# Splitting 16 rows off the second load of a single-core transpose, into two transfers of 8 rows

## The chip, the cores and the metric

The kernel runs on one core of a Trainium2 chip. The metric is the device time of one execution in microseconds (us). The kernel before was run twice: 1261.91 and 1262.47 us, median 1262.19 us. A profiled execution of the same kernel is read below; its span, from the first to the last instruction of the program, is 1260.4 us.

## The reference

```python
def setup_inputs():
    return {"x": np.random.randn(8192, 8192).astype(np.float32)}

def reference(x):
    return np.transpose(x)
```

The input has 8192 x 8192 float32 values, 268.4 MB. All of it is read once from HBM and all of it written once, transposed.

## The kernel before

**Tiling.** The input is cut into 128 chunks. Chunk t is a pair (s, c): s is one of two halves of 4096 columns, c one of 64 blocks of 128 rows. A chunk is a tile of 128 partitions with 4096 float32 each; one row of it in one partition has 16 KB, the whole tile 2 MB. `load(t)` (L101) brings it into one of three input buffers, `ins[t % 3]`. The first three loads are issued on SyncE's queue, all later ones on ScalarE's queue (L103).

**Transposing.** For each chunk TensorE does 32 transposes of 128 x 128 (`transposes`, L112), in eight groups q of four. The first four groups land in the first half of PSUM, the last four in the second half. A group takes every fourth column, so partition p of the result holds four neighbouring rows of the output. TensorE runs this as a loop in hardware registers (L130 to L140).

**Copying and storing.** ScalarE copies the first half of PSUM and VectorE the second half into one of nine regions of `regs` in SBUF (L241). A region is a window of up to eight chunks for one q: 128 partitions, four output rows each, up to 1024 columns, so 2 MB when full. Windows are staggered (L198), so that from the start one window closes with each chunk; the first ones and the last ones are shorter. A closed window is stored by `store` (L154), always from ScalarE's queue; every store but the first goes through the helper `wide_dma` (L25), which builds the transfer by hand.

**What orders the work.** Each engine has its own stream, and semaphores tie them. `s_ld[k]` (one for each input buffer) gets 16 from a landed load, one increment for each transfer engine, and one each from ScalarE's and VectorE's last copy of the chunk before. TensorE takes a chunk when it reads 18 and subtracts 18 (L113). For chunk 0 the two copies are replaced by plain increments (L96, L97). `s_pe` counts TensorE's progress for the copies and for ScalarE, which issues the store of a closed window and then `load(t + 3)` into the buffer that TensorE has finished. `s_st[r]` counts the landed stores of region r; a copy that opens a new window waits for it. At the end SyncE waits for the stores of all nine regions (L266).

Of the kernel before, what the change touches and what calls it, by code (L numbers as in the profile page):

```python
# [8 lines left out]
def physical(ap):  # L9


    t = ap.tensor
    dims = [list(d) for d in ap.ap]
    if len(dims) == 2:
        dims.insert(1, [dims[1][1], 1])
    return mybir.PhysicalAccessPattern(
        ap=dims,
        offset=ap.offset,
        dtype=ap.dtype,
        memref=t.name,  # L20
        memsetref=t.name + "_set",
    )


def wide_dma(nc, eng, queue, out, in_):  # L25


    return eng.add_instruction(
        mybir.InstDMACopy(
            mode="Copy",  # L30
            name=nc.get_next_instruction_name(),
            engine=eng.engine,
            ins=[physical(in_)],
            outs=[physical(out)],
            queue=queue,
        )
    )
# [3 lines left out]
def kernel(  # L41
# [13 lines left out]
    nc = tc.nc  # L55
    P = 128
# [8 lines left out]
    NIN = 3  # L65
    NREG = 9
    CH = N // P
    J = S * P

    with tc.tile_critical():  # L70
        nc.alloc_sbuf_tensor("pad", [P, 32], dt)
        ident = nc.alloc_sbuf_tensor("ident", [P, P], dt).ap()
        ins = [nc.alloc_sbuf_tensor(f"in{k}", [P, J], dt).ap() for k in range(NIN)]
        SIZE = B * W * P
# [4 lines left out]
        s_id = nc.alloc_semaphore("s_id")  # L79
        s_ld = [nc.alloc_semaphore(f"s_ld{k}") for k in range(NIN)]  # L80
        s_st = [nc.alloc_semaphore(f"s_st{k}") for k in range(NREG)]
        s_pe = nc.alloc_semaphore("s_pe")
        s_cp = [nc.alloc_semaphore("s_cpa"), nc.alloc_semaphore("s_cpv")]

# [3 lines left out]
            out=ident,  # L88
            in_=ident,
# [8 lines left out]

        chunks = [(s, c) for s in range(M // J) for c in range(CH)]

        def load(t):  # L101
            s, c = chunks[t]
            (nc.sync if t < NIN else nc.scalar).dma_start(  # L103
                out=ins[t % NIN], in_=x[c * P:(c + 1) * P, s * J:(s + 1) * J]
            ).then_inc(s_ld[t % NIN], 16)

# [34 lines left out]
        for t in range(NIN):  # L143
            load(t)

        copied = [0, 0]
        free = list(range(NREG))
        stored = [0] * NREG
        window = {}

        def later(t):
            return W <= t < T - NIN

        def store(q, e, t):  # L154
            t0, r, parts = window.pop(q)
            if later(t):
                nc.scalar.wait_ge(s_pe, (t + 1) * NH + 1)
            else:
                nc.scalar.wait_ge(s_cp[e], copied[e])
            base = 0  # L160
            pieces = []
            for s, a, z in parts:
                rows = (z - a) * P
                j0 = s * J + q * B * P
                dst = out[j0:j0 + B * P, a * P:a * P + rows]
                dst = dst.rearrange("(q b) i -> q b i", q=P)
                src = regs[:, r * SIZE + base:r * SIZE + base + B * rows]
                base += B * rows
                pieces.append((rows, dst, src))
            for rows, dst, src in sorted(pieces, key=lambda v: -v[0]):  # L170
                if any(stored):
                    st = wide_dma(nc, nc.scalar, "qActDynamicHW", dst, src)
                else:
                    st = nc.scalar.dma_start(
                        out=dst, in_=src.rearrange("q (b i) -> q b i", b=B)
                    )
                st.then_inc(s_st[r], 16)
                stored[r] += 1
            free.append(r)

        def closes(w, t):
            t0, r, parts = w
            return t + 1 == t0 + sum(z - a for _, a, z in parts)

        for t, (s, c) in enumerate(chunks):
            closed = []
            for e in range(2):
                eng = (nc.scalar, nc.vector)[e]
                go = s_ld[(t + 1) % NIN]

                place = []
                fresh = {}
                for q in range(e * NH, (e + 1) * NH):
                    if q not in window:

                        span = (q - c) % W + 1  # L198
                        r = free.pop(0)
                        parts = [(s, c, min(c + span, CH))]  # L200
                        if c + span > CH and t + span < T:
                            parts.append((s + 1, 0, c + span - CH))
                        window[q] = (t, r, parts)
                        if stored[r]:
                            fresh[q - e * NH] = (s_st[r], 16 * stored[r])
                    t0, r, parts = window[q]
                    k = [p[0] for p in parts].index(s)
                    base = r * SIZE + B * P * sum(z - a for _, a, z in parts[:k])
                    _, a, z = parts[k]
                    place.append((base + (c - a) * P, (z - a) * P))  # L210

                runs = []
                for g in range(NH):
                    if runs:
                        u = runs[-1]
                        gap = place[g][0] - place[g - 1][0]
                        if place[g][1] == place[u[0]][1] and abs(gap) < 2 ** 15 and (
                            len(u) == 1 or gap == place[u[1]][0] - place[u[0]][0]
                        ):
                            u.append(g)  # L220
                            continue
                    runs.append([g])
                if later(t):
                    runs = sorted(runs, key=lambda u: any(g in fresh for g in u))
                seen = t * NH + e * NH // 2
                for u in runs:
                    off, dist = place[u[0]]
                    gap = place[u[-1]][0] - place[u[-2]][0] if len(u) > 1 else 0
                    dims = [list(regs.ap[0]), [gap, len(u)], [dist, B], [1, P]]
                    o = bass.AP(regs.tensor, regs.offset + off, dims)  # L230
                    i = pss[e][:, u[0] * B * P:(u[-1] + 1) * B * P]
                    i = i.rearrange("p (l b i) -> p l b i", b=B, i=P)
                    need = t * NH + (e * NH + u[-1]) // 2 + 1
                    if later(t) and u is runs[0] and len(runs) > 1 and any(g in fresh for g in runs[-1]):
                        need = t * NH + (e * NH + max(v[-1] for v in runs)) // 2 + 1
                    if need > seen:
                        eng.wait_ge(s_pe, need)
                        seen = need
                    for sem, value in [fresh[g] for g in u if g in fresh]:
                        eng.wait_ge(sem, value)  # L240
                    cp = nc.scalar.copy(out=o, in_=i) if e == 0 else nc.vector.tensor_copy(out=o, in_=i)  # L241
                    ends = [e * NH + g for g in u if closes(window[e * NH + g], t)]
                    if later(t):
                        if u is runs[-1]:
                            cp.then_inc(go, 1)
                        closed += [(q, e) for q in ends]
                        continue
                    if ends:
                        cp.then_inc(s_cp[e], 1)
                        copied[e] += 1  # L250
                    if u is runs[-1]:
                        if ends:
                            eng.wait_ge(s_cp[e], copied[e])
                            eng.sem_inc(go, 1)
                        else:
                            cp.then_inc(go, 1)
                    for q in ends:
                        store(q, e, t)
            for q, e in closed:
                store(q, e, t)  # L260
            if t + NIN < T:
                if not closed:
                    nc.scalar.wait_ge(s_pe, (t + 1) * NH)
                load(t + NIN)
        for r in range(NREG):
            nc.sync.wait_ge(s_st[r], 16 * stored[r])  # L266


# [28 lines left out]
```

## Time and profile before

| what | value |
|---|---|
| median of two runs | 1262.19 us (1261.91 to 1262.47) |
| span of the profiled execution | 1260.4 us |
| TensorE matmul busy | 739.0 us, 59% |
| VectorE busy | 302.0 us, 24% |
| ScalarE busy | 253.5 us, 20% |
| bytes moved by transfers | 536.95 MB, 426 GB/s over the span |
| ScalarE's transfer queue (q10) | 530.60 MB, 99.0% of 16 engines' span |
| SyncE's transfer queue (q1) | 6.29 MB, 1.2% |

The profiled execution has no time of its own beside its span; the span stands 1.8 us under the median of the runs, which time the whole execution from outside.

A profile row for a group of instructions reads: line, engine, operation, out<-in, count, then busy time and mean. A row of a table of stretches gives the stretch, its length, the busy time of each engine with its count of instructions, the granted TensorE clock, the mean busy share of the 16 transfer engines, and the GB/s moved. In that table a transfer packet is counted, whole, where it starts. A row of the timeline gives start, length, engine, line, operation and count, and in brackets how long the engine had been idle and what ended that. "ACTq" and "SPq" are the instruction queues of ScalarE and SyncE.

### The profile page before, as it was taken

How to read it: one execution, taken by the hardware profiler on the slowest of the kernel's cores; microseconds unless marked ns; L12 is line 12 of the kernel's file. 1: busy time of each engine (PE TensorE's matmuls, PEld its weight loads, DVE VectorE, ACT ScalarE, POOL GpSimd, SP SyncE). 2: the span in 40 equal slices, each digit the busy share in tenths (PEclk: the TensorE clock that was granted, in tenths of full speed). 3: DMA queues.
4: the chain of work that ended last, by engine and by line, in shares of the span. 5: the costliest groups of instructions: out<-in, count | busy, mean ns of one | idle time of the engine just before them, and what ended most of it. 6: DMA issues, size and time to landing. Idle time of an engine off the chain costs nothing. (4 is left out here: it accounts for less than half of the span.)

```text
span 1260.4 us, 9367 instructions
## 1 busy us (share of the span) xinstructions
PE 739.0 (59%) x4096; PEld 718.4 (57%) x4096; DVE 302.0 (24%) x250; ACT 253.5 (20%) x257; POOL 0.7 (0%) x6
## 2 busy tenths in 40 slices
PE   5656556565566655565556656566565655665561
PEld 5556556565556655565555656565565655665561
DVE  2322222222222222222222222222222222222220
ACT  3212211122111211122111211121111211121110
POOL 0000000000000000000000000000000000000000
PEclk9886876868777777778687786867777687777776
DMA  9999999999999999999999999999999999999998
GB/s 383 429 422 426 425 430 431 426 431 431 427 430 431 428 428 431 428 429 432 427 422 426 429 429 425 431 429 428 430 428 428 431 428 429 429 429 429 429 431 376
DMA packets 39271, 536.95 MB, mean 426 GB/s; under 512 B 4320, under 2 KB 4832, under 8 KB 6240
## 3 DMA queue, kind: packets, MB, share of 16 engines
q10 hardware_dynamic: 38832, 530.60, 99.0%
q1 hardware_dynamic: 432, 6.29, 1.2%
q14 instruction: 6, 0.05, 0.0%
q8 instruction: 1, 0.02, 0.0%
HBM read 268.44 MB, written 268.44 MB: 426 GB/s over the span
## 5 line engine op out<-in xcount | busy, mean ns | idle before, releaser
L117 PE MATMUL ps<-ident,in 128*128 128x128 f32 x4096 | 739.0, 362 | 493.5 <-PEq L113 493.5
L117 PEld LDWEIGHTS ps<-ident,in 128*128 128x128 f32 x4096 | 718.4, 220 | 513.9 <-issue 513.9
L241 DVE COPY regs<-ps 128x512 f32<-128x512 f32 (+3 forms) x250 | 302.0, 1246 | 932.1 <-PE ps L117 932.1
L241 ACT COPY regs<-ps 128x512 f32<-128x512 f32 (+3 forms) x256 | 252.2, 1016 | 978.8 <-PE ps L117 760.8
L241 ACT ACT_TABLE_LOAD x1 | 1.3, 1283 | 1.0 <-SPq L70 1.0
L87 POOL TENSOR_SCALAR_AFFINE_SELECT ident<-ident 128x128 f32<-128x128 f32 x1 | 0.3, 293 | 0.2 <-POOL ident L85 0.2
L85 POOL MEMSET ident<- 128x128 f32 x1 | 0.2, 204 | 0.5 <-SPq L70 0.5
L281 POOL MEMSET const-bfloat16-1.0<- 128x1 bf16 x1 | 0.1, 102 | 0.0
L281 POOL MEMSET const-uint8-127<- 128x1 uint8 x1 | 0.1, 102 | 0.0
L281 POOL MEMSET const-float32-0.0<- 128x1 f32 x1 | 0.1, 99 | 0.2 <-issue 0.2
L281 POOL MEMSET const-float32-1.0<- 128x1 f32 x1 | 0.1, 99 | 0.0
## 6 DMA issues: line engine op xcount, KB each, us to landing
in<-in_x_dram ACTq DMA_DIRECT2D x125, 2048.0 KB, 16.8
out_dram<-regs ACTq DMA_DIRECT2D x114, 2048.0 KB, 12.6
out_dram<-regs ACTq DMA_DIRECT2D x4, 1792.0 KB, 11.1
in<-in_x_dram SPq DMA_DIRECT2D x3, 2048.0 KB, 11.7
out_dram<-regs ACTq DMA_DIRECT2D x4, 1536.0 KB, 12.5
out_dram<-regs ACTq DMA_DIRECT2D x4, 1280.0 KB, 11.5
out_dram<-regs ACTq DMA_DIRECT2D x4, 1024.0 KB, 11.1
out_dram<-regs ACTq DMA_DIRECT2D x4, 768.0 KB, 12.3
```

The costliest lines, as they stand in the source:

```text
L85: nc.gpsimd.memset(ident, 0.0).then_inc(s_id, 1)
L87: nc.gpsimd.affine_select(out=ident, in_=ident, compare_op=mybir.AluOpType.not_equal, fill=1.0, base=0, pattern=[[-1, P]], channel_multipl ...
L117: tr = nc.tensor.transpose(pss[e][:, (g * B + b) * P:(g * B + b + 1) * P], ins[k][:, q * B * P + b:(q + 1) * B * P - B + b + 1:B], ident,)
L241: cp = nc.scalar.copy(out=o, in_=i) if e == 0 else nc.vector.tensor_copy(out=o, in_=i)
L281: nc = _bacc.Bacc("TRN2", target_bir_lowering=False, num_devices=1)
```

## The change

Only the load of chunk 1, one of the three that SyncE issues at the start, is cut. Its first 112 rows stay one transfer on SyncE's queue. Rows 112 to 119 go in a transfer on SyncE's queue, rows 120 to 127 in one on ScalarE's queue. Both are built by `wide_dma` with the source seen as 4 x 2 rows. They count on a semaphore of their own, `s_ex`. VectorE waits for 32 on it ahead of its last copy of chunk 0; the increment of that copy is one of those that TensorE needs before it takes chunk 1. Besides, the wait for the region stored last moves at the very end of the program from SyncE to VectorE.

```diff
+    EXTRA = [(4, 2), (4, 2)]
...
+        s_ex = nc.alloc_semaphore("s_ex")
...
         def load(t):
             s, c = chunks[t]
+            src = x[c * P:(c + 1) * P, s * J:(s + 1) * J]
+            a = P - sum(e * n for e, n in EXTRA) if t == 1 else P
             (nc.sync if t < NIN else nc.scalar).dma_start(
-                out=ins[t % NIN], in_=x[c * P:(c + 1) * P, s * J:(s + 1) * J]
+                out=ins[t % NIN][:a], in_=src[:a]
             ).then_inc(s_ld[t % NIN], 16)
+            if t == 1:
+                for (e, n), (eng, queue) in zip(EXTRA, ((nc.sync, "qSPDynamicHW"), (nc.scalar, "qActDynamicHW"))):
+                    part = src[a:a + e * n].rearrange("(e n) j -> e n j", e=e)
+                    wide_dma(nc, eng, queue, ins[t][a:a + e * n], part).then_inc(s_ex, 16)
+                    a += e * n
...
+                    if t == 0 and e == 1 and u is runs[-1]:
+                        eng.wait_ge(s_ex, 16 * len(EXTRA))
                     cp = nc.scalar.copy(out=o, in_=i) if e == 0 else nc.vector.tensor_copy(out=o, in_=i)
...
         for r in range(NREG):
-            nc.sync.wait_ge(s_st[r], 16 * stored[r])
+            (nc.vector if r == free[-1] else nc.sync).wait_ge(s_st[r], 16 * stored[r])
```

In the order of the built program, SyncE issues the load of chunk 0, the 112 rows, the first 8 rows, then the load of chunk 2. ScalarE issues the second 8 rows as its very first transfer, ahead of its function table load and its first copy. Nothing else moves on any engine.

## The prediction

> **What bounds the kernel now.** I read the page first: the span, the line of slices for the transfers, the queues and the transfer issues.
>
> ```profile
> span 1260.4 us, 9367 instructions
> ...
> DMA  9999999999999999999999999999999999999998
> ...
> q10 hardware_dynamic: 38832, 530.60, 99.0%
> q1 hardware_dynamic: 432, 6.29, 1.2%
> ...
> in<-in_x_dram ACTq DMA_DIRECT2D x125, 2048.0 KB, 16.8
> out_dram<-regs ACTq DMA_DIRECT2D x114, 2048.0 KB, 12.6
> ...
> in<-in_x_dram SPq DMA_DIRECT2D x3, 2048.0 KB, 11.7
> ```
>
> All 40 slices are full: the 16 transfer engines are busy from one end to the other, and 99.0% + 1.2% of their time is packets. A load lands 16.8 us after its issue, though 2 MB cost far less (next view): it stands behind other transfers. So the kernel is bound by its transfers, and the change neither adds nor removes a byte. What can move is which of the 16 engines carries which row. The next view is the table of stretches, for the middle and the last microseconds.
>
> ```profile
> 200.00:500.00 300.00, 182.52 (x992) 177.53 (x992) 72.60 (x54) 59.64 (x48) 0.00 (x0) 0.74 1.01 429
> ...
> 1255.12:1255.72 0.60, 0.00 (x0) 0.00 (x0) 0.00 (x0) 0.00 (x0) 0.00 (x0) 0.50 1.03 437
> 1255.72:1256.33 0.61, 0.00 (x0) 0.00 (x0) 0.00 (x0) 0.00 (x0) 0.00 (x0) 0.50 0.89 376
> 1256.33:1256.94 0.61, 0.00 (x0) 0.00 (x0) 0.00 (x0) 0.00 (x0) 0.00 (x0) 0.50 0.63 269
> 1256.94:1257.55 0.61, 0.00 (x0) 0.00 (x0) 0.00 (x0) 0.00 (x0) 0.00 (x0) 0.50 0.32 134
> 1257.55:1258.15 0.60, 0.00 (x0) 0.00 (x0) 0.00 (x0) 0.00 (x0) 0.00 (x0) 0.50 0.26 109
> 1258.15:1258.76 0.61, 0.00 (x0) 0.00 (x0) 0.00 (x0) 0.00 (x0) 0.00 (x0) 0.50 0.00 0
> ```
>
> In the middle 429 GB/s over 16 engines are 26.8 GB/s for each, so a row of 16 KB (16,384 B) takes one engine 0.61 us. That is the length of the late slices, so an engine that still has work starts one packet in each. Shares times 16 give the engines still at work: 16, 14, 10, 5, 4, 0. The engines do not end together: two stop four slices (2.4 us) ahead of the last four. **The end is set by those four**, and by the closing behind them:
>
> ```profile
> L266 SPq EVENT_SEMAPHORE  x4: 27/28/4912, 1250.4 to 1254.3; - x4
> ```
>
> SyncE's last wait begins at 1254.3 and takes 4.9 us, so the last store has landed at 1259.2; 1.2 us of closing follow to 1260.4.
>
> **The change part by part.**
>
> *Rows per engine.* Before, an engine carries 128/16 = 8 rows of load 1. After, 112/16 = 7, which is 0.61 us less for each. The 16 other rows go to engines four at a time, two rows each. Nothing in the trace shows a transfer four engines wide, so I take both ends: the two transfers use the same four engines, which then have 7 + 4 = 11 rows (+3 rows, +1.83 us) while twelve have -0.61 us; or different fours, and eight engines have 9 rows (+0.61 us) and eight 7. As no engine waits for work afterwards (below), such an offset stays to the end, where only the last engine counts. With the same four the end moves, by slices: +1.8 us if one of the last four engines is among them; +1.2 if the latest of them is the fifth; +0.6 if it is one of the five that stop two slices early; 0 for those three slices early; at best -0.6. Were any four of 16 equally likely, one of the last four would be in in 73 of 100 draws (1 - 495/1820). With different fours it is +0.6 almost surely. I take the middle of the two likeliest, **+1.2 us**, and keep -0.6 and +1.8 as ends.
>
> The trace does not say which engines a narrow transfer takes. [...] No row here numbers the engines.
>
> *The start.* The rows:
>
> ```profile
> 0.94 1.32 SPq L103 DMA_DIRECT2D in<-in_x_dram  x3
> ...
> 0.98 1.28 ACT L241 ACT_TABLE_LOAD   x1 [0.98 <-SPq L70]
> ...
> 8.40 5.50 PE L117 MATMUL ps<-ident,in 128*128 128x128 f32 x32 [8.40 <-PEq L113]
> 10.39 0.58 ACT L241 COPY regs<-ps 128x512 f32<-128x512 f32 x1 [8.13 <-PE ps L117]
> 11.01 0.63 ACTq L174 DMA_DIRECT2D out_dram<-regs  x1
> ...
> 12.97 2.48 DVE L241 COPY regs<-ps 128x512 f32<-128x512 f32 x4 [12.97 <-PE ps L117]
> 13.94 0.36 ACTq L103 DMA_DIRECT2D in<-in_x_dram  x1
> ...
> 15.60 4.11 PE L117 MATMUL ps<-ident,in 128*128 128x128 f32 x32 [1.70 <-PEq L113]
> ```
>
> SyncE issues four transfers, not three: 1.32/3 = 0.44 us more, which puts load 2's issue at some 2.3 us. Cover: loads 0 and 1 occupy the engines until 13.1 us (issue of the middle load about 1.4 + 11.7). Cost nothing; without the cover, 0.44 us. ScalarE's new issue costs 0.4 to 0.63 us (its first two issues above) ahead of the table load, which then ends near 2.9 us instead of 2.26; ScalarE has nothing to do before 10.39. Cost nothing; uncovered, 0.6 us.
>
> ScalarE's 8 rows are not queued behind load 0: they are on the other queue and ready at the same time. If an engine serves both queues in turn, load 0 is two rows (1.2 us) late on the four engines and TensorE starts at 9.6. All of ScalarE's first issues then move by 1.2 us: the first store to 12.2, load 3 to 15.2. Cover: loads 1 and 2 last until about 18.0 (4.9 us for each load), so load 3 is in the queue 2.8 us ahead of need, the first store 5.8 us. Cost nothing; without cover up to 1.2 us.
>
> *The added wait.* VectorE waits for both short transfers ahead of its fourth copy of chunk 0, at 12.97 + 3 x 0.62 = 14.8 us; behind it are the increment that TensorE needs for chunk 1 (15.60) and all of VectorE's later copies. SyncE's 8 rows land after at most 3 more rows than load 1 before: 13.1 + 1.8 = 14.9. If load 0 was late the copy is due at 16.0, and the wait is over; if not, it costs 0.1 us. Ends: 0 and 1.8 us (nothing late, everything queued badly), value 0; it would be TensorE's delay, not the queues', with the cover just named.
>
> *The middle.* Whether a lead of one engine starves it, read from the timeline of two chunks:
>
> ```profile
> 493.65 5.26 PE L117 MATMUL ps<-ident,in 128*128 128x128 f32 x32 [3.23 <-PEq L113]
> 495.63 0.55 ACTq L28 DMA_DIRECT2D out_dram<-regs  x1
> 496.22 0.61 ACTq L103 DMA_DIRECT2D in<-in_x_dram  x1
> ...
> 503.40 5.47 PE L117 MATMUL ps<-ident,in 128*128 128x128 f32 x32 [4.48 <-PEq L113]
> 505.38 0.55 ACTq L28 DMA_DIRECT2D out_dram<-regs  x1
> ```
>
> A chunk takes 9.75 us. TensorE begins when the last engine has landed its load; 2.0 us later ScalarE issues a store, in 0.55 us. Between these the engine that was last works on the store and load behind it, 9.75 us of work. So an engine may lead by 9.75 - 2.0 - 0.55 = 7.2 us, less the way from issue to first packet, before it runs dry. That way is at most 2.5 us (at the start TensorE begins 7.46 us after load 0's issue, and its 8 rows take 4.9 of these), which leaves at least 4.7. Before, the lead at the end is 2.4 us; after, at most 2.4 + 2.4 = 4.8. And where a leader did run dry it would lose only its lead; the last engine always has work.
>
> *The closing.* VectorE takes the wait for the region stored last; SyncE's other eight waits are done earlier. An elapsed wait costs SyncE 0.03 us (the 27/28 ns above), and the whole closing is 1.2 us. Gain between 0 and 1.2, nearest to the small row with the signal behind it: 0.2 us.
>
> **Sum:** 1260.4 + 1.2 - 0.2 = 1261.4 us of span; with the 1.8 us that lie around the span, **1263.2 us**. That is 0.1% over the median.
>
> **Rivals.**
>
> *The early engines take the rows.* If the four engines are those that finish first, the last four save a row: -0.6, with the closing -0.2 to -0.8. Time 1261.4 to 1262.0. For it: 11 of 16 engines stop at least 1.2 us ahead of the last. Against: all four must be early.
>
> *Not four wide.* If each short transfer ran on one engine, the same for both, that engine has 7 + 16 rows, +15 x 0.61 = +9.2 us: 1271. If the 112 rows went on fewer engines, say eight, these get 14 rows: +6 x 0.61 = +3.7 us. For it: no transfer of 8 or 112 rows is in the trace. Against: the source is laid out as 4 x 2.
>
> *Slower, by starving.* In the middle, if the larger spread passed the 4.7 us and the engines that run dry held up the rest, each of some 118 later chunks would pay what is over: at 1 us, 118 us and 1380. It decides from a lead of 4.7 us at the earliest; I get 4.8 at most, and see no way in which the last engine pays.
>
> *Other stalls.* The engines' order shifts by up to 2.4 us against each other, which could change how they hinder each other in memory.
>
> ```profile
> 4.00:8.00 4.00, 0.00 (x0) 0.00 (x0) 0.00 (x0) 0.00 (x0) 0.00 (x0) 1.00 1.02 438
> ```
>
> Load 0 alone ran at 438 GB/s. At that rate all 536.95 MB take 1226 us: the far end of a gain, 34 us. Loads and stores together ran at 429; a change of a tenth of that gap is 3 us, either way: 1259 to 1266.
>
> **How the numbers follow.** Forecast (the end moves by 0 to +1.8 us less the closing; 1262.0 to 1263.9): 0.60. Early engines: 0.22. Other stalls, beyond these: 0.11. Not four wide: 0.05. Starving: 0.02. The range reaches over the first two and most of the stalls: 1260.6 to 1265.2. A difference of 2% (25 us), about what a measurement of this kernel can tell from no change, is passed only by starving and by the far end of the stalls: faster 0.01, same 0.97, slower 0.02.
>
> **What the profile after would show.** Queue q1 with 128 KB less than 6.29 MB (8 of 384 rows on q10). The short transfers landing well before 16 us; TensorE's first matmul near 9.6 if the queues are served in turn, 8.4 if not; full transfer slices throughout. In the last slices a longer tail: some engines done about 0.6 us earlier, up to four 1.8 us later; if the tail is shorter than 2.4 us, the early engines took the rows. The closing nearer to 1.0 than 1.2 us. I am wrong if the late slices look as before and the time moves by over 3 us: then the rate in the middle has changed.

## The result, and the profile after

The changed kernel takes 1271.84 us, the median of 1270.82 and 1272.85, against 1262.19 before: a ratio of 1.0076, 95% interval 1.0047 to 1.0105. That is 9.65 us more, within 2% but clear of the spread of the runs, and outside the range that was given. The profiled execution, the longer of the two, went from a span of 1260.4 to 1271.1 us, 10.7 more; the profile below is of that one.

The page of the changed kernel:

```profile
span 1271.1 us, 9370 instructions
...
DMA  9999999999999999999999999999999999999998
GB/s 270 420 428 430 431 430 430 429 430 429 429 430 430 430 430 432 428 428 430 430 413 423 430 429 429 429 428 430 430 430 429 430 429 430 429 429 428 426 422 355
...
q10 hardware_dynamic: 38844, 530.73, 98.3%
q1 hardware_dynamic: 428, 6.16, 1.9%
```

All slices of the transfer line are full, as before; by busy share nothing has changed. The line under it tells more: the first slice moved only 270 GB/s (383 before), the middle runs at 428 to 430 as it did. The engines were busy in that first slice, but with packets that took longer. q1 has 128 KB less, as it should, yet its share of time rose from 1.2% to 1.9%. The table of stretches shows where, first the kernel before, then the changed one (last column: GB/s, the one ahead of it: busy share of the transfer engines):

```profile
8.00:13.00 5.00, 4.60 (x26) 4.63 (x27) 0.03 (x1) 1.89 (x4) 0.00 (x0) 1.00 0.98 419
13.00:18.00 5.00, 3.30 (x28) 3.14 (x27) 2.46 (x4) 1.33 (x3) 0.00 (x0) 1.00 0.98 401
18.00:25.00 7.00, 5.30 (x44) 5.14 (x43) 2.89 (x5) 2.80 (x6) 0.00 (x0) 1.00 1.07 415
```

```profile
4.00:8.00 4.00, 0.00 (x0) 0.00 (x0) 0.00 (x0) 0.00 (x0) 0.00 (x0) 1.00 1.02 324
8.00:13.00 5.00, 0.14 (x1) 0.17 (x2) 0.00 (x0) 0.00 (x0) 0.00 (x0) 1.00 1.08 236
13.00:18.00 5.00, 5.00 (x25) 5.00 (x26) 0.00 (x0) 2.15 (x4) 0.00 (x0) 1.00 0.97 239
18.00:25.00 7.00, 1.13 (x11) 0.97 (x9) 2.58 (x4) 0.00 (x0) 0.00 (x0) 0.74 0.99 226
...
500.00:1200.00 700.00, 418.31 (x2284) 406.87 (x2285) 167.26 (x137) 138.99 (x138) 0.00 (x0) 0.75 1.01 428
```

From 4 to 25 us the engines are as busy as ever and move 60% of what they moved before. Against the kernel before (438, 419, 401, 415) the stretches lack 114 x 4 + 183 x 5 + 162 x 5 + 189 x 7 = 3504 KB, which at 429 GB/s are **8.2 us**. The rest of the run is unchanged: from 500 to 1200 us the rate is 428, against 429 before. The same in the records of the landings, where each transfer gives one increment for each of its engines (16 records for a load, four for a narrow transfer); the times are those of the first and of the last engine, in us:

| | load 0 | load 1 (its ordinary part) | load 2 | last store |
|---|---|---|---|---|
| before | 7.9 to 8.3 | 12.8 to 13.1 | 17.8 to 18.1 | 1256.5 to 1259.2 |
| changed | 10.3 to 12.7 | 17.8 to 20.6 | 26.1 to 28.9 | 1265.1 to 1269.9 |

The first engine is 8.3 us late with load 2 and 8.6 at the end; the last engine 10.7 both times. The loss of the first engine is all there before chunk 3. The last engine's delay is smaller in between: from load 10 to load 60 it is 7.8 to 8.6 us, since by load 10 the kernel before has a spread of 3.1 us of its own. The start of the timeline:

```profile
0.98 1.28 ACTq L28 DMA_DIRECT2D in<-in_x_dram  x1
...
1.86 0.81 SPq L28 DMA_DIRECT2D in<-in_x_dram  x1
...
12.86 6.22 PE L126 MATMUL ps<-ident,in 128*128 128x128 f32 x32 [12.86 <-PEq L122]
...
18.17 1.89 DVE L252 COPY regs<-ps 128x512 f32<-128x512 f32 x3 [18.17 <-PE ps L126]
...
24.12 0.69 DVE L252 COPY regs<-ps 128x512 f32<-128x512 f32 x1 [4.07 <-DMA in<-in_x_dram]
24.96 5.41 PE L126 MATMUL ps<-ident,in 128*128 128x128 f32 x32 [5.87 <-PEq L122]
```

TensorE begins at 12.86 us, not at 8.40. VectorE waits 4.07 us for the short transfers, and TensorE takes chunk 1 at 24.96, not at 15.60. This wait cost nothing that can be seen: load 2 occupies the engines until 26 to 29 us, load 3 was issued at 19.12, and no later load has the first engine more than 8.3 us late. The last slices of the changed kernel:

```profile
1263.93:1264.54 0.61, 0.00 (x0) 0.00 (x0) 0.00 (x0) 0.00 (x0) 0.00 (x0) 0.50 1.01 426
1264.54:1265.14 0.60, 0.00 (x0) 0.00 (x0) 0.00 (x0) 0.00 (x0) 0.00 (x0) 0.50 0.52 219
1265.14:1265.75 0.61, 0.00 (x0) 0.00 (x0) 0.00 (x0) 0.00 (x0) 0.00 (x0) 0.50 0.44 188
1265.75:1266.36 0.61, 0.00 (x0) 0.00 (x0) 0.00 (x0) 0.00 (x0) 0.00 (x0) 0.50 0.44 188
1266.36:1266.96 0.60, 0.00 (x0) 0.00 (x0) 0.00 (x0) 0.00 (x0) 0.00 (x0) 0.50 0.45 191
1266.96:1267.57 0.61, 0.00 (x0) 0.00 (x0) 0.00 (x0) 0.00 (x0) 0.00 (x0) 0.50 0.32 134
1267.57:1268.18 0.61, 0.00 (x0) 0.00 (x0) 0.00 (x0) 0.00 (x0) 0.00 (x0) 0.50 0.32 134
1268.18:1268.79 0.61, 0.00 (x0) 0.00 (x0) 0.00 (x0) 0.00 (x0) 0.00 (x0) 0.50 0.07 27
```

Eight engines start no packet after 1264.5, five are still at work in the slice from 1267.6. The tail has grown from 2.6 us (1256.5 to 1259.2) to 4.8.

### The profile page after: what moved, and what is told of

Its sections match the earlier page's. It is cut to its first block, busy times and chain, and to the rows that moved or that the text cites. A ratio compares the mean times of both kernels' runs of the same rounds, so it can differ in the third digit from the quotient of the medians.

```text
span 1271.1 us, 9370 instructions
## 1 busy us (share of the span) xinstructions
PE 742.1 (58%) x4096; PEld 721.5 (57%) x4096; DVE 302.0 (24%) x250; ACT 253.6 (20%) x257; POOL 0.7 (0%) x6
## 6 DMA issues: line engine op xcount, KB each, us to landing
out_dram<-regs ACTq DMA_DIRECT2D x4, 1536.0 KB, 11.7
out_dram<-regs ACTq DMA_DIRECT2D x4, 768.0 KB, 13.1
```

## The experiments

**The theories.** The narrow transfers and the 112 rows differ from an ordinary load in three ways: in how they are built (hand-made, narrow), in what they read, and in which partitions they write. Theory P says it is the place: engines that write neighbouring partitions at the same time hinder each other. The runs vary the place of a transfer; which partition an engine writes, no trace shows. A group, in the expectations, is four neighbouring partitions; that such groups count is the author's assumption. P's rivals are N (the narrow, hand-made form), H (the 112-row shape, or uneven shares) and the reading side (HBM, engines out of step).

**1. The narrow transfers alone.** Load 1 stays whole. The narrow transfers read their rows again, into a region of `regs` that is free at that time and where nothing uses them (a dummy run); so 16 rows more are moved than the reference needs. This is the edit against the changed kernel:

```diff
-            a = P - sum(e * n for e, n in EXTRA) if t == 1 else P
+            a = P
...
             if t == 1:
-                for (e, n), (eng, queue) in zip(EXTRA, ((nc.sync, "qSPDynamicHW"), (nc.scalar, "qActDynamicHW"))):
+                a = P - sum(e * n for e, n in EXTRA)
+                views = [regs[112 + 8 * i:120 + 8 * i, 8 * SIZE:9 * SIZE] for i in range(2)]
+                for i, ((e, n), (eng, queue)) in enumerate(zip(EXTRA, ((nc.sync, "qSPDynamicHW"), (nc.scalar, "qActDynamicHW")))):
...
-                    wide_dma(nc, eng, queue, ins[t][a:a + e * n], part).then_inc(s_ex, 16)
+                    wide_dma(nc, eng, queue, views[i], part).then_inc(s_ex, 16)
```

> Load 1 stays one transfer of 128 rows; the two narrow transfers read the same 16 rows again, into partitions 112 to 127 of a region of regs that is still free, so 256 KB are moved more and the 112-row transfer is gone. The added bytes alone put 4 rows of 0.61 us on each of four engines: 0 to +2.4 us at the end. Theory P (the place in SBUF: engines that write neighbouring partitions at the same time hinder each other, and with them all 16): the narrow transfers are slow as in the changed kernel, stretches of 8 to 13 us and 18 to 25 us fall to 300 GB/s or less where they are in flight, load 1 alone runs at about 430; some 6 us are lost (3.2 beside load 0, 2.8 beside load 2), 1268 to 1271 us. Theory N (the narrow hand-built form itself, wherever it writes): the same, 1268 to 1271. Theory H (the 112-row transfer is what is slow): 1262 to 1265, no stretch under 400 GB/s.

Measured: 1268.66 us, ratio 1.0055 (1.0038 to 1.0071). The table of stretches:

```profile
4.00:8.00 4.00, 0.00 (x0) 0.00 (x0) 0.00 (x0) 0.00 (x0) 0.00 (x0) 1.00 1.02 328
8.00:13.00 5.00, 1.08 (x5) 1.11 (x6) 0.00 (x0) 0.00 (x0) 0.00 (x0) 1.00 1.02 334
13.00:18.00 5.00, 5.00 (x29) 4.96 (x27) 0.76 (x2) 2.15 (x4) 0.00 (x0) 1.00 1.16 341
18.00:25.00 7.00, 3.63 (x19) 3.51 (x18) 1.81 (x3) 1.07 (x2) 0.00 (x0) 0.67 0.90 323
```

The loss comes in two pieces with full speed between them: between 10.5 and 15 us the packets of load 1 take 0.61 us again. The first engine is done with load 0 at 9.9 us and with load 2 at 22.4, 4.6 later than before. So the 112 rows are not all of it; P and N stand. The rates stayed a little above the 300 GB/s that was expected of both.

**2. The same, into every second partition,** 0 to 14 and 1 to 15.

```diff
-                views = [regs[112 + 8 * i:120 + 8 * i, 8 * SIZE:9 * SIZE] for i in range(2)]
+                views = [regs[i:i + 15:2, 8 * SIZE:9 * SIZE] for i in range(2)]
```

> [...] Theory P: nothing is slow, no stretch under 400 GB/s after the first 3 us; only the added bytes, 1262 to 1265 us. Theory N, and any theory that blames the reading side in HBM or the engines being out of step: as with adjacent partitions, 1268 to 1271. Theory H: 1262 to 1265, as with adjacent partitions.

Measured: 1263.12 us, ratio 1.0015 (1.0005 to 1.0025).

```profile
4.00:8.00 4.00, 0.00 (x0) 0.00 (x0) 0.00 (x0) 0.00 (x0) 0.00 (x0) 1.00 1.01 434
8.00:13.00 5.00, 3.56 (x17) 3.59 (x18) 0.00 (x0) 0.86 (x2) 0.00 (x0) 1.00 1.00 426
13.00:18.00 5.00, 3.30 (x25) 3.14 (x24) 2.48 (x4) 1.29 (x3) 0.00 (x0) 1.00 1.00 391
18.00:25.00 7.00, 5.29 (x45) 5.13 (x44) 2.48 (x4) 3.08 (x6) 0.00 (x0) 1.00 1.03 386
```

Nothing is slow beside load 0. From 13 us the rate is 391 and 386, under the 400 GB/s of the expectation, where the kernel before has 401 and 415; this small rest is not explained. The first engine is done with load 2 at 17.8 us, to the tenth as before. Same bytes, rows, queues and form, another place, and the loss is gone: this **rules out N and the reading side** for the narrow transfers, and shows that for them it is the place. How the place does it, as P has it or otherwise, is not shown. What is left, 1.5 us, lies within the 2.4 us of the four rows more on four engines.

**3. The 112 rows alone.** No narrow transfer; the 16 rows go in one ordinary transfer.

```diff
-                for (e, n), (eng, queue) in zip(EXTRA, ((nc.sync, "qSPDynamicHW"), (nc.scalar, "qActDynamicHW"))):
-                    part = src[a:a + e * n].rearrange("(e n) j -> e n j", e=e)
-                    wide_dma(nc, eng, queue, ins[t][a:a + e * n], part).then_inc(s_ex, 16)
-                    a += e * n
+                nc.sync.dma_start(out=ins[t][a:], in_=src[a:]).then_inc(s_ex, 16)
...
-                        eng.wait_ge(s_ex, 16 * len(EXTRA))
+                        eng.wait_ge(s_ex, 16)
```

> 112 rows, and the other 16 rows in one ordinary transfer on SyncE's queue, 16 engines wide, one row each; no narrow transfer is left. Theory P: the 112 rows are slow as in the changed kernel (7 rows at 1.07 us and not 0.61, 3.2 us lost), and the 16 rows, four engines to a group of four partitions, cost some 1.8 us more: about 1267 us, a stretch near 240 GB/s between 8 and 16 us. Theory H: 3.2 us lost, 1265 to 1266. Theory N: nothing lost, 1262 us, full rate throughout.

Measured: 1265.34 us, ratio 1.0029 (1.0018 to 1.0040), 3.7 us over the runs beside it.

```profile
4.00:8.00 4.00, 0.00 (x0) 0.00 (x0) 0.00 (x0) 0.00 (x0) 0.00 (x0) 1.00 1.00 426
8.00:13.00 5.00, 4.70 (x22) 4.73 (x23) 0.00 (x0) 1.99 (x4) 0.00 (x0) 1.00 1.09 311
13.00:18.00 5.00, 1.62 (x12) 1.43 (x10) 2.58 (x4) 0.15 (x1) 0.00 (x0) 0.90 0.92 218
```

The 112 rows run at 311 GB/s, the 16 rows behind them slower still. The first engine is done with load 2 at 21.6 us, 3.8 late. Together with the 4.6 of the narrow transfers that is 8.4, against the 8.3 of the changed kernel. The near agreement is partly chance. Here the 112 rows lose some 2.1 us (packets of 0.75 to 1.1 us up to 13 us) and the 16 rows behind them 1.6, which the changed kernel does not have; there the 112 rows lose some 3.2 (0.9 to 1.2 us each). Why they are slower there is open. The size lies nearer to H than to P's own 1267, so the next run tells these two apart.

**4. Two transfers of 64 rows.** The kernel of experiment 3 with 64 rows cut off in place of 16: two ordinary transfers, 16 engines wide, even shares of four rows, nothing narrow.

```diff
-    EXTRA = [(4, 2), (4, 2)]
+    EXTRA = [(8, 4), (8, 4)]
```

> Load 1 as two ordinary transfers of 64 rows (partitions 0 to 63, then 64 to 127) on SyncE's queue, nothing narrow; each is 16 engines wide with four rows, so every engine still carries eight rows. If only engines that write the same four neighbouring partitions hinder each other, nothing is shared here: 1262 us, load 1 at 430 GB/s. [...] If uneven shares (7 rows) were what slowed the 112 rows, 1262.

Measured: 1266.82 us, ratio 1.0040 (1.0023 to 1.0057).

```profile
8.00:13.00 5.00, 4.18 (x22) 4.21 (x23) 0.00 (x0) 1.47 (x3) 0.00 (x0) 1.00 0.99 210
13.00:18.00 5.00, 1.45 (x12) 1.25 (x11) 1.89 (x3) 0.68 (x2) 0.00 (x0) 1.00 0.97 210
```

Half the speed of before, to the point: 210 and 419 GB/s. Even shares do not help, so H falls as the one explanation; that the 112 rows are slow by their place is the simplest reading, but no run moves them. Nor does a run here keep the rows that are read and move only the place, as experiment 2 did. Nor did the expectation's other 1262 us come out, that of four neighbouring partitions. Why 64 rows run at half the speed, no run shows.

**5. Every second partition, in another place.** The dummy rows again, into every second partition from 112. "The own groups" of the expectation are the run of experiment 2.

```diff
-                views = [regs[112 + 8 * i:120 + 8 * i, 8 * SIZE:9 * SIZE] for i in range(2)]
+                views = [regs[112 + i:127 + i:2, 8 * SIZE:9 * SIZE] for i in range(2)]
```

> Again the same bytes and queues as the two dummy runs, load 1 whole. [...] Theory M (a group of partitions takes one row in 0.61 us whoever writes it, and all 16 engines go at the pace of the fullest group): 2 rows more in a group for each narrow transfer, so 1.2 us lost beside load 0 and 1.2 beside load 2, where four rows a group (adjacent partitions) lost 2.4 and some 3; 1265 to 1266 us, between the 1263.1 of the own groups and the 1268.7 of the adjacent ones. Theory S (only engines of one and the same transfer hinder each other): nothing lost, 1263.

Measured: 1266.74 us, ratio 1.0036 (1.0020 to 1.0052).

```profile
4.00:8.00 4.00, 0.00 (x0) 0.00 (x0) 0.00 (x0) 0.00 (x0) 0.00 (x0) 1.00 1.07 365
8.00:13.00 5.00, 2.20 (x11) 2.23 (x12) 0.00 (x0) 0.22 (x1) 0.00 (x0) 1.00 0.97 347
13.00:18.00 5.00, 3.89 (x23) 3.70 (x21) 1.89 (x3) 1.93 (x4) 0.00 (x0) 1.00 1.04 311
```

The first engine is done with load 2 at 21.0 us, 3.2 late, between 0.0 in experiment 2 and 4.6 in experiment 1; beside SyncE's rows, which landed at 18.5 to 18.8, packets take up to 1.25 us, twice 0.61. The stepping is that of experiment 2 and only the place is another, and 3.2 us are lost in place of 0.0: S, which had nothing lost, falls. Something else acts as well. Between 10.5 and 15 us ScalarE's rows have landed, SyncE's have not begun, and the packets of load 1 still take 0.70 us on all engines. That is 0.8 of the 3.2 us, and no theory here has it.

**6. What holds the engines that carry no narrow row?** In experiments 1 and 5 all 16 engines are slow, though a narrow transfer has only four of them. Three dummy runs, one execution each, vary how many engines a narrow transfer has and how many partitions it fills: two engines and four partitions, two and eight, four and four. The edit is against experiment 1; the first and the third write 112 to 115 and 120 to 123.

```diff
-    EXTRA = [(4, 2), (4, 2)]
+    EXTRA = [(2, 2), (2, 2)]
...
+    EXTRA = [(2, 4), (2, 4)]
...
+    EXTRA = [(4, 1), (4, 1)]
```

> Narrow transfers of 4 rows, two engines wide, each into one group of four partitions (112 to 115, and 120 to 123), load 1 whole: half the bytes of the adjacent run, and one group hit by each in place of two. Theory M: a group still gets 4 rows more, so all 16 engines lose as much as with adjacent partitions: load 0 has its first engine done some 2.4 us late, the packets beside the narrow transfers take 1.1 us and more on every engine, 1267 to 1269 us. If instead each hit group slows only its own share of the engines, half of it: 1265, and most packets stay at 0.61 us.

> [...] Two groups are hit by two narrow engines, where the one-group run had two narrow engines on one group and left 13 engines at full rate. If the number of groups hit decides whether all 16 engines are slowed: load 0's first engine is done at 9.5 us or later and packets beside ScalarE's rows take some 1.2 us on all engines. If the number of narrow engines decides: most packets stay near 0.61 us and 13 or 14 engines finish load 0 at 8.1 to 8.4 us. The end is late by the eight rows more on two engines in either case: 1266 to 1272 us.

> Four rows in each narrow transfer, four engines with one row each, all into one group of four partitions (112 to 115, 120 to 123); load 1 whole. If the number of narrow engines decides: all 16 engines are slowed as with adjacent partitions, load 0's first engine done at 9 us or later. If the number of groups decides: as the one-group run, 11 or more engines finish load 0 at 8.1 to 8.4 us. The end: 2 rows more on four engines, 1263 to 1266 us.

| each narrow transfer | load 0 done, by engine | time, one run |
|---|---|---|
| two engines, four partitions | thirteen at 8.1 to 8.4, three at 10.5 to 11.4 | 1271.99 |
| two engines, eight partitions | fourteen at 8.8 to 9.5, two at 12.8 | 1285.56 |
| four engines, four partitions | all at 9.8 to 10.5 | 1265.64 |

With two engines on four partitions 13 engines keep their pace (8.1 to 8.4; 7.9 to 8.3 before); with four on the same four, all 16 are late by 2 us. So theory M, that everyone goes at the pace of the fullest group, is wrong as it stood; nor does the number of partitions or that of narrow engines alone decide. The same number of both does not give the same loss either: the first engine is 2.0 us late with load 0 in experiment 1, and only 1.1 in experiment 5. What holds up the engines that carry no narrow row is **open**. The times of two of these runs lie far over what was expected. A single time says little, since one of 23 executions of the kernel before beside experiment 1 took 1270.29 us; but their profiles show where the time went, and experiment 8 takes that up.

**7. Twice the rows, and dealt out alternately.** The first is a dummy run with `EXTRA = [(4, 4), (4, 4)]` into partitions 112 to 127 and 96 to 111. The second is the changed kernel itself with its 16 rows dealt alternately to the two queues, so that a transfer fills every second partition:

```diff
-                    part = src[a:a + e * n].rearrange("(e n) j -> e n j", e=e)
-                    wide_dma(nc, eng, queue, ins[t][a:a + e * n], part).then_inc(s_ex, 16)
-                    a += e * n
+                    part = src[a:a + 15:2].rearrange("(e n) j -> e n j", e=e)
+                    wide_dma(nc, eng, queue, ins[t][a:a + 15:2], part).then_inc(s_ex, 16)
+                    a += 1
```

> [...] Theory M: still 4 rows more in a group, so the loss of all engines is as with adjacent partitions, some 5 to 6 us; the eight rows more on four engines add up to 4.9 us at the end: 1270 to 1273. If the loss goes with the bytes of the narrow transfers, 11 to 12 us are lost before chunk 3 and the time is over 1276.

> The changed kernel, but the 16 rows are dealt out alternately: rows 112, 114 to 126 go on SyncE's queue, 113, 115 to 127 on ScalarE's. The 112-row transfer stays. Theory M: two rows a group and transfer in place of four, so 2.4 to 3 us less than the changed kernel: 1268 to 1269.5. Theory S: the narrow transfers lose nothing, 1265 to 1266. If neither counts and the narrow form itself is slow: as the changed kernel, 1271 to 1272.

Measured: with twice the rows 1275.52 us in one execution, and the first engine done with load 2 at 22.4 us, 4.5 late. That is as late as in experiment 1 with half the rows, but the place differs too (96 to 127, there 112 to 127), so two things differ. Against experiment 5, with half the rows and every second partition from 112, it is 4.5 for 3.2. How the early loss goes with the rows alone, these runs do not tell. The time lies between the 1273 of M and the 1276 of the loss by bytes. The alternate rows gave 1270.95 us, ratio 1.0085 (1.0054 to 1.0116), with runs from 1268.69 to 1276.98: too scattered to stand apart from the changed kernel. Its profile (the run of 1268.69) has load 2 done by the first engine at 23.6 us, 2.5 us sooner than in the changed kernel, as M has it; the median missed its 1268 to 1269.5.

**8. A lead without an early loss.** As the run with twice the rows, but into partitions 0 to 15 and 32 to 47, where the author expected no early loss. Eight rows more on each of four engines, at 0.61 us, are an estimated 4.9 us of lead.

```diff
-                views = [regs[112 - 16 * i:128 - 16 * i, 8 * SIZE:9 * SIZE] for i in range(2)]
+                views = [regs[32 * i:32 * i + 16, 8 * SIZE:9 * SIZE] for i in range(2)]
```

> [...] Place theory: packets stay at 0.61 us in the first 14 us, load 2's first engine is done at 17.8 us as before, the last at about 23. What becomes of so large a lead is the second question: if a lead costs nothing but itself, as the prediction had it, the time is 1264 to 1267 us and the rate between 500 and 1200 us stays at 428 to 429 GB/s; if leads over some 5 us starve the engines again and again, as the runs with two engines on two groups and with 16 rows suggest, the rate there falls to 421 to 427 and the time is over 1268.

Measured: 1268.85 us, ratio 1.0054 (1.0037 to 1.0071). The stretches of this run, and one of the kernel before:

```profile
4.00:8.00 4.00, 0.00 (x0) 0.00 (x0) 0.00 (x0) 0.00 (x0) 0.00 (x0) 1.00 1.02 438
8.00:13.00 5.00, 2.48 (x12) 2.52 (x13) 0.00 (x0) 0.49 (x1) 0.00 (x0) 1.00 0.99 423
...
200.00:400.00 200.00, 116.72 (x640) 113.49 (x640) 48.60 (x34) 38.75 (x32) 0.00 (x0) 0.76 1.01 422
400.00:600.00 200.00, 120.36 (x656) 117.16 (x657) 47.56 (x41) 38.97 (x38) 0.00 (x0) 0.75 1.01 429
```

```profile
200.00:400.00 200.00, 121.28 (x659) 118.09 (x660) 46.70 (x32) 38.99 (x33) 0.00 (x0) 0.75 1.01 429
```

The first 13 us are at the speed of before (438 and 423) though twice the rows go narrow, and load 2's first engine is done at 17.7 us: the place once more. But the time is over 1268. The lead, the time between the first and the last engine, is 6.1 us at load 2. Between 200 and 400 us the rate is 422 and not 429, which makes 7/429 x 200 = 3.3 us; by chunk 60 the first engine has lost 4.2 us, and the lead is 4.6. It came earlier than the expectation had it (500 to 1200 us stayed at 429). The run of experiment 6 with two engines and eight partitions shows two kinds of loss:

```profile
25.00:50.00 25.00, 18.31 (x132) 17.66 (x131) 9.94 (x16) 8.45 (x14) 0.00 (x0) 0.92 0.92 366
...
600.00:800.00 200.00, 116.05 (x640) 112.83 (x640) 47.65 (x51) 39.52 (x46) 0.00 (x0) 0.76 1.01 421
800.00:1000.00 200.00, 116.40 (x640) 113.17 (x640) 46.71 (x28) 39.52 (x40) 0.00 (x0) 0.76 1.00 421
1000.00:1200.00 200.00, 120.39 (x640) 117.17 (x640) 47.34 (x37) 38.34 (x27) 0.00 (x0) 0.72 1.01 421
```

From 25 to 50 us the busy share is 0.92: engines do run dry. The first engine's delay grows from 4.1 us (load 2) to 7.3 (load 5), and that of the last does not (9.1 and 8.9). From 600 us on the rate is 421, against 427 to 429 in the kernel before, which is 1.4 to 1.9% less, and the first and the last engine fall back together. There the busy share is 1.00 to 1.01, as in the kernel before and in the slow stretch of experiment 8, so no engine is seen to stand idle. It is the packets that take longer: a load's packet takes 0.624 us on average between 200 and 400 us in experiment 8, 0.614 in the kernel before.

This second loss goes with the lead. In these traces, between 50 and 600 and between 700 and 1200 us, every stretch of 50 us with a mean lead over 5.5 us ran at 418 to 423 GB/s; between 4.8 and 5.5 there are slow stretches and whole ones. The changed kernel has a lead of 2.6 to 4.4 us up to chunk 60 and 3.6 to 5.5 after, and its rate (428) is all but whole. That the lead makes the packets longer, and how, is not shown.

**9. The closing alone.** The kernel before with the last wait moved, nothing else.

```diff
-            nc.sync.wait_ge(s_st[r], 16 * stored[r])
+            (nc.vector if r == free[-1] else nc.sync).wait_ge(s_st[r], 16 * stored[r])
```

> The kernel before with only the last wait moved from SyncE to VectorE. All theories of the start: no change there. From the prediction the closing is 0.2 us shorter: 1262.0 us, no difference that can be measured. The time from the last landing to the end of the span goes from 1.2 to about 1.0 us.

Measured: 1262.07 us, ratio 1.0005 (0.9985 to 1.0026): no difference. In the trace the time from the last landing to the end of the span goes from 1.27 to 1.16 us.

## Why the prediction was wrong

*What bounds the kernel* held: the transfers do, from end to end, and the last engine sets the end.

*Rows per engine* is **the step that failed**. It priced every row at 0.61 us, whichever engine carries it and wherever it lands, from stretches in which all engines carry ordinary transfers. The count of rows was right; the price was not. In the changed kernel a row beside ScalarE's narrow transfer or of the 112 rows takes 0.9 to 1.7 us, beside SyncE's narrow transfer up to 2.1, and all 16 engines are late by it. That is 8.3 us for the first engine: 2.4 in load 0, 2.6 in load 1 (with a row less), 3.3 in load 2. For the narrow transfers, so for loads 0 and 2, experiments 1, 2 and 8 show that the place of the rows makes it. For the 112 rows it is argued from experiments 3 and 4. Why engines that carry no narrow row are held up too is open.

The part of the step on the engines' shares came out, by the end that the prediction kept and not by its middle value of 1.2: the transfers are four engines wide (q10 has 12 packets up to 13 us, eight rows and four increments), and the spread at load 2 is 2.7 us where the same four engines with three rows more against one less make 2.4. With 8.3 for everyone this gives the 10.7 us of the last engine. That both narrow transfers use the same four is read from the landings of load 2: twelve engines are done at 26.1 to 26.6 us, four at 28.7 to 28.9.

*The start*: the issues cost nothing, as forecast, but were mis-sized; ScalarE's took 1.28 us for an estimated 0.4 to 0.63. TensorE began at 12.86, not at 9.6, for the reason above. The short transfers were to land well before 16 us; ScalarE's landed at 11.7 us, SyncE's at 24.1. *The added wait* was put at 0, at most 1.8 us; it took 4.07, and cost nothing that can be seen, with the cover that was named.

*The middle*: that a leader which runs dry "would lose only its lead" came out where engines ran dry, from 25 to 50 us in the second run of experiment 6: the first engine lost 3.2 us, the last nothing. What the prediction did not have is a loss with busy engines: in the same run the last engine, too, lost 1.4 to 1.9% for hundreds of microseconds. It goes with leads of some 5 us and more, near the prediction's 4.7, but that is luck: the 4.7 was worked out for engines that run dry, and none is seen to do so there. In the changed kernel it hardly mattered.

*The closing* was put at 0.2 us and measures 0.1.

*Rivals*: "not four wide" had 1271 us, almost the measured time, by a mechanism that did not happen; that is luck. "Other stalls" came nearest in kind, but was bounded by 3 us either way and looked for in the middle, in memory. That a transfer that isn't 128 rows can halve the speed (64 rows: 210 for 419 GB/s, experiment 4) was on no list. The prediction's sign of being wrong did not point there either: it had late slices as before and a changed rate in the middle, and the runs have late slices that changed and a middle that did not.

## What to carry to other kernels

Before a transfer is cut, look at the partitions where its rows land, not only at how many an engine carries: 64 rows, 112 rows, and 8 rows put into partitions 112 to 127 were slower for each row than 128 rows (0.61 us), by some 1.2 to 3.4 times, and the 8 rows slowed what ran beside them. The same 8 rows in partitions 0 to 15 were not slow (experiment 2). Read the GB/s line next to the busy line: slow packets count as busy (here from 4 to 25 us, a busy share of 0.97 to 1.08 at 226 to 324 GB/s). A term for which the trace has no instance (here: any transfer that is not 128 rows) deserves the wide range, not the confident price of its neighbour.

## What the runs showed of the hardware that was not expected

- A narrow transfer can hold up engines that carry none of its rows: with two engines on four partitions, 13 engines kept 8.1 to 8.4 us for load 0; with four engines on the same four, all 16 took 9.8 to 10.5. Why is open.
- A narrow transfer of 8 rows holds its issuing queue longer than a load of 128 rows: 1.28 us on ScalarE and 0.81 on SyncE, against 0.38 to 0.41 for SyncE's others. Whether its width, its form or being first makes it, no run tells. ScalarE's rows began to move at 5.8 us, 3.5 us after their issue had ended.
- The 16 engines are not in step. In the kernel before the lead of the first over the last grows from 0.3 us at load 2 to 3.1 at load 10 and is 2.6 at the last load. Stretches with a mean lead over 5.5 us ran at 418 to 423 GB/s in place of 429, with a busy share as before (experiment 8).
